# Softmax heads of a hybrid decoder layer: scores computed twice, per 512 queries, and no transposes of the weights

## The chip, the core and the metric

The kernel runs on one core of one Trainium2 chip. The metric is the device time of one execution in microseconds (us), the median of several runs. A core has a matrix engine (TensorE: PE for its matmuls, PEld for the weight loads of the same queue), VectorE (DVE), ScalarE (ACT), GpSimd (POOL) and SyncE (SP), which here issues the DMAs. Every engine works through its own list of instructions in order, and waits on semaphores for the others.

## The reference

One decoder layer over 2048 tokens of width 1024, in float32. A combined projection feeds four mixers: A stick-breaking attention (4 heads of 64), B a gated MLP, C an RWKV-7 recurrence, D forgetting attention (4 heads of 64). Their outputs go through `w_out`, then a mixture of 32 experts and a last norm. The change concerns D alone, which for each head computes

```python
logits = einsum('bhqd,bhkd->bhqk', q, k) * scale
logits = logits + cum[q] - cum[k]          # cumulative log forget gate
probs  = softmax(where(k <= q, logits, -inf))
out    = einsum('bhqk,bhkd->bhqd', probs, v)
```

## The kernel before

The program runs the input projection, then RWKV (C) together with the two attentions (A, then D), then the output projection with the router, then the experts. The order of the instructions on each engine is fixed when the program is built: a scheduler takes the code of RWKV and of the attentions and lays them into one another, so each engine's list in this part alternates between pieces of both. It knows no more than what the code's tiles depend on and its own idea of how long things take.

The softmax heads (D) are handled in blocks `b` of 256 queries, two tiles `i` of 128 queries each. For a tile the method `softmax` goes over the keys in pieces `c` of 512 (`spans`). `logits` writes a bank `z` of PSUM with queries on the partitions and keys along the row: one matmul of `qs` (stationary) with `kh`, one with `kl`, both float32r, and on the diagonal a 128-wide bf16 matmul (L378) that adds the mask. `kh` and `kl` are the rounded key and its remainder; `qs` holds the rounded query in its upper and the remainder in its lower 64 rows. One DVE operation (L402) scales the bank, adds the key's gate `nk`, writes the result `S` to SBUF and keeps the running maximum `m`. After the last piece two small DVE operations make the bias (L408, L409), ACT takes the exponential of every piece in place and sums the row (L413), and DVE forms the reciprocal (L416).

Then `weigh` treats the keys two tiles (`p`) at a time: three or four 128x128 transposes by the matrix engine (L425) bring the weights to keys on the partitions, ACT copies them to SBUF (`tq`, L427), and two float32 matmuls (L431) with the 64-wide `v` as stationary tile write the even keys to partitions 0 to 63 of `o` and the odd keys to 64 to 127. `out` adds the two halves and multiplies by the reciprocal, which two more transposes (L455) lay along the row. `logits` and `weigh` also serve the stick-breaking heads (A). While the matmuls of one block's `weigh` run, the next block's logits are made.

`load` brings a 512-token piece of `q`, `k`, `v` and the gate by DMA and splits them on POOL (L344, L345, L350, L351, L366).

Of the kernel before, what the change touches and what calls it, by code (L numbers as in the profile page):

```python
# [8 lines left out]
F32 = mybir.dt.float32  # L9
# [11 lines left out]
NT = 16  # L21
W = 256
NH = 4
# [284 lines left out]
def attention(tc, K, ctx, sT, sV, cumD, mixT):  # L308
# [13 lines left out]

    def bank():
        return ps.tile([128, 512], F32, name="bk", tag="bk")

    class Head:
        def __init__(self, h, sb):
            self.h, self.sb = h, sb
            self.q0, self.k0, self.v0 = (0, 256, 0) if sb else (512, 768, 256)
            self.q0, self.k0, self.v0 = (a + h * HD for a in (self.q0, self.k0, self.v0))  # L330
            self.kh, self.kl, self.qs, self.v, self.nk = [], [], [], [], []
            if sb:
                self.vc = cp.tile([64, NT], F32, name="vc", bufs=2)
                with nc.allow_non_contiguous_dma(reason="small"):
                    nc.sync.dma_start(self.vc, dram(sV, 127 * 516 + self.v0, [[1, HD], [128 * 516, NT]]))

        def load(self, c):
# [16 lines left out]
            if self.sb:  # L354
                u = rp.tile([128, 4, HD], F32, name="u")
# [15 lines left out]
        def logits(self, i, c, w):  # L371
            q = self.qs[i // 4][:, (i % 4) * 128:(i % 4) * 128 + 128]
            last = c == i // 4
            z = bank()
            nc.tensor.matmul(z[:, :w], q, self.kh[c][:, :w], start=True, stop=False)  # L375
            nc.tensor.matmul(z[:, :w], q, self.kl[c][:, :w], start=False, stop=not last)  # L376
            if last:
                nc.tensor.matmul(z[:, w - 128:w], K.identb, K.sb_mask if self.sb else K.fx_mask, start=False, stop=True)  # L378
            return z[:, :w]

        def spans(self, i):
            n = (i + 1) * 128
            return [(c, c * 512, min(512, n - c * 512)) for c in range(i // 4 + 1)]
# [11 lines left out]

        def softmax(self, i, S, rq):
            mx = None
            for c, x0, w in self.spans(i):
                z = self.logits(i, c, w)
                S[c] = sp.tile([128, 512], F32, name="S", tag="S")  # L400
                m = tp.tile([128, 1], F32, name="m")
                nc.vector.tensor_tensor_reduce(S[c][:, :w], z, self.nk[c][:, :w], 0.125,  # L402
                                               -3.0e38 if mx is None else mx, op0=OP.add, op1=OP.max, accum_out=m)
                mx = m
                yield
            c1 = cq[:, i, self.h:self.h + 1]
            bias = tp.tile([128, 1], F32, name="bias")
            nc.vector.tensor_add(bias, mx, c1)  # L408
            nc.vector.tensor_sub(bias, c1, bias)  # L409
            sm = tp.tile([128, 4], F32, name="sm")  # L410
            n = i // 4 + 1
            for c, x0, w in self.spans(i):
                nc.scalar.activation(S[c][:, :w], S[c][:, :w], AF.Exp, bias=bias, accum_out=sm[:, c:c + 1])  # L413
            if n > 1:
                nc.vector.tensor_reduce(sm[:, 0:1], sm[:, 0:n], AX.X, OP.add)
            nc.vector.reciprocal(rq, sm[:, 0:1])  # L416
# [17 lines left out]
        def out(self, b, o, rq):  # L434
            ol = op.tile([64, 256], F32, name="ol")
            oo = op.tile([64, 256], F32, name="oo")
            if self.sb:
                for a in range(2):
                    s = slice(a * 128, a * 128 + 128)
                    c = self.vc[:, 2 * b + a:2 * b + a + 1]  # L440
                    if a or b:
                        nc.scalar.activation(ol[:, s], o[64:128, s], AF.Identity, bias=c)
                    else:
                        nc.vector.tensor_copy(ol[:, s], c.to_broadcast([64, 128]))
                nc.vector.tensor_add(oo, o[0:64], ol)
                nc.sync.dma_start(mixT[self.h * HD:self.h * HD + HD, b * 256:b * 256 + 256], oo)
                return
            if b:
                nc.scalar.activation(ol, o[64:128], AF.Copy)
            else:  # L450
                nc.vector.memset(ol[:, 0:128], 0.0)
                nc.scalar.activation(ol[:, 128:256], o[64:128, 128:256], AF.Copy)
            t = bank()
            for a in range(2):
                nc.tensor.transpose(t[:, a * 128:a * 128 + 128], rq[:, a:a + 1].to_broadcast([128, 128]), K.ident)  # L455
            nc.vector.tensor_add(oo, o[0:64], ol)
            nc.vector.tensor_mul(oo, t[0:64, 0:256], oo)
            r0 = 768 + self.h * HD
            nc.sync.dma_start(mixT[r0:r0 + HD, b * 256:b * 256 + 256], oo)

        def block(self, b):
            S = [{}, {}]
            rq = None if self.sb else tp.tile([128, 2], F32, name="rq")
            o = []

            def weigh(p, first, last):
                if first:
                    o.append(po.tile([128, 256], F32, name="o"))
                self.weigh(b, p, S, o[0], first, last)
                if last:  # L470
                    self.out(b, o[0], rq)
# [14 lines left out]
            def front0():  # L486
                if b % 2 == 0:
                    self.load(b // 2)
                yield from self.softmax(2 * b, S[0], rq[:, 0:1])

            def mid():
                yield from self.softmax(2 * b + 1, S[1], rq[:, 1:2])

            def back0():
                for p in range(b + 1):
                    weigh(p, p == 0, p == b)
                    yield

            if self.sb:
                return [([front(c)], [], back(c)) for c in range(b // 2, -1, -1)]  # L500
            return [([front0()], [mid()], back0())]

    prev = iter(())
    for sb in (True, False):
        for h in range(NH):
            H = Head(h, sb)
            for b in range(8):
                for first, second, back in H.block(b):
                    for g in first:
                        yield from g  # L510
                    for g in second:
                        for _ in prev:
                            yield
                            next(prev, None)
                            next(g, None)
                        yield from g
                    yield from prev
                    prev = back
    yield from prev
# [1356 lines left out]
```

## Time and profile before

| | before |
|---|---|
| median of 3 runs (lowest to highest) | 2599.4 us (2596.69 to 2601.01) |
| profiled execution, first to last instruction | 2606.8 us |
| mean granted TensorE clock of it | 0.967 of full speed |
| busy share PE / PEld / DVE / ACT / POOL | 94% / 67% / 64% / 51% / 26% |

The times of the runs and the profiled execution are separate executions: the profiled one took 2606.8 us, 7.4 us (0.3%) over the median. A busy share is an average over stages with different limits. The softmax heads stand from about 1060 to 1522 us of the profiled execution, with RWKV's second half laid between them; the output projection's first matmul starts at 1526.3 us.

### The profile page before, as it was taken

To read this page: it belongs to the slowest core of one execution; us is meant where nothing else is said; L and a number is where in the kernel's file an instruction comes from. 1 tells how busy PE (TensorE), PEld (TensorE's weight loads), DVE (VectorE), ACT (ScalarE), POOL (GpSimd) and SP (SyncE) were. 2 spreads that over 40 slices of the span, in tenths; PEclk is the share of its full clock that TensorE was granted. 3 is DMA by queue.
4 is the path that set the end of the run, shared out by engine and by line. 5 is a ranking of instruction groups with operands and counts; after the bars stand their busy time and mean duration, and the time that the engine had idled before them with its cause. 6 is when DMAs were issued, how large, how long until landed. Compare 5 with 4: busy or idle time off the path is not lost. (4 is left out here: it accounts for less than half of the span.)

```text
span 2606.8 us, 42226 instructions
## 1 busy us (share of the span) xinstructions
PE 2442.3 (94%) x14802; PEld 1754.4 (67%) x14803; DVE 1675.3 (64%) x3881; ACT 1324.1 (51%) x2527; POOL 675.1 (26%) x691
## 2 busy tenths in 40 slices
PE   7999999997989898999999998997999999999994
PEld 6789998874656564656556667774666666676663
DVE  5313402247797869687685756665677787787885
ACT  5201222224655565675565642223667677776774
POOL 2000000015464647331332022112212232222224
PEclk9999999998989999999999999998999999999997
DMA  8510222125120211111111059443989899899995
GB/s 245 174 59 30 77 69 69 63 67 118 34 60 26 48 41 39 46 55 41 49 32 43 11 187 275 130 122 111 337 271 331 306 329 368 308 321 358 327 317 164
DMA packets 241826, 394.73 MB, mean 151 GB/s; under 512 B 65921, under 2 KB 106753, under 8 KB 241608
## 3 DMA queue, kind: packets, MB, share of 16 engines
q1 hardware_dynamic: 222472, 336.68, 39.1%
q0 software_dynamic: 19136, 55.30, 7.5%
q8 instruction: 118, 1.93, 0.3%
q14 instruction: 100, 0.82, 0.1%
HBM read 319.24 MB, written 76.85 MB: 152 GB/s over the span
## 5 line engine op out<-in xcount | busy, mean ns | idle before, releaser
L72 DVE TENSOR_TENSOR wl<-wr,wh 128x1024 fp32r<-128x1024 f32 x366 | 442.6, 1223 | 114.5 <-ACT wh L71 107.6
L71 ACT ACTIVATE wh<-wr 128x1024 fp32r<-128x1024 f32 x366 | 381.6, 1057 | 138.0 <-PE pg L1446 53.8
L393 DVE TENSOR_TENSOR_SCAN S<-S,zero 128x512 f32<-128x512 f32 (+3 forms) x160 | 197.8, 1246 | 50.5 <-POOL S L391 50.3
L152 PE MATMUL p<-hhi,wh 128*128 128x512 f32 x512 | 206.1, 404 | 14.8 <-ACT hhi L112 6.9
L425 PE MATMUL bk<-ident,S 128*128 128x128 f32 x1088 | 186.3, 292 | 24.5 <-DVE S L393 18.5
L427 ACT ACTIVATE tq<-bk 128x512 f32<-128x512 f32 (+1 forms) x288 | 156.6, 571 | 101.0 <-PE bk L425 81.4
L154 PE MATMUL p<-hhi,wl 128*128 128x512 f32 x512 | 205.2, 401 | 0.0
L153 PE MATMUL p<-hlo,wh 128*128 128x512 f32 x512 | 204.9, 400 | 0.0
L431 PE MATMUL o<-tq,v 128*64 128x256 f32 (+1 forms) x1152 | 189.3, 400 | 4.3 <-ACT tq L427 2.8
L425 PEld LDWEIGHTS bk<-ident,S 128*128 128x128 f32 x1088 | 124.0, 145 | 98.3 <-issue 53.4
L156 DVE TENSOR_TENSOR e<-p,rb 128x512 f32<-128x512 f32 x64 | 43.6, 689 | 198.3 <-PE p L154 183.9
L391 POOL TENSOR_SCALAR S<-S 128x512 f32<-128x512 f32 (+3 forms) x160 | 127.9, 808 | 145.8 <-ACT S L390 129.8
L735 POOL TENSOR_TENSOR k<-big,k 128x512 f32<-128x512 f32 x8 | 14.2, 1774 | 554.8 <-DVE big L734 548.8
L375 PE MATMUL bk<-kh,qs 128*128 128x512 f32 (+2 forms) x320 | 147.7, 462 | 7.2 <-POOL qs L351 4.8
L171 PE MATMUL p<-wh,hhi 128*128 128x256 f32 (+1 forms) x512 | 144.6, 282 | 0.0
L172 PE MATMUL p<-wl,hhi 128*128 128x256 f32 (+1 forms) x512 | 144.3, 282 | 0.0
L173 PE MATMUL p<-wh,hlo 128*128 128x256 f32 (+1 forms) x512 | 143.7, 281 | 0.0
L152 PEld LDWEIGHTS p<-hhi,wh 128*128 128x128 f32 x512 | 97.9, 191 | 40.2 <-ACT hhi L112 6.5
L413 ACT ACTIVATE S<-S,bias 128x512 f32<-128x512 f32 (+3 forms) x160 | 103.6, 649 | 34.2 <-DVE bias L409 33.7
L376 PE MATMUL bk<-kl,qs 128*128 128x512 f32 (+2 forms) x320 | 120.9, 379 | 0.0
L71 ACT ACTIVATE wh<-raw 128x512 fp32r<-128x512 f32 (+1 forms) x52 | 27.6, 589 | 179.2 <-PE p L153 171.7
L1443 PE MATMUL pg<-wh,xh 128*128 128x512 f32 x248 | 102.6, 414 | 12.6 <-ACT s L1450 12.6
(559 smaller groups left out, 6144.6 us busy)
## 6 DMA issues: line engine op xcount, KB each, us to landing
wr<-in SPq DMA_DIRECT2D x386, 512.0 KB
raw<-in SPq DMA_DIRECT2D x108, 256.0 KB
sT<-e SPq DMA_DIRECT2D x64, 256.0 KB
raw<-sT SPq DMA_DIRECT2D x128, 128.0 KB
mr<-mixT SPq DMA_DIRECT2D x16, 512.0 KB
xt<-in SPq DMA_DIRECT2D x16, 512.0 KB
xacc<-xt SPq DMA_DIRECT2D x16, 512.0 KB
h2D<-h SPq DMA_DIRECT2D x16, 512.0 KB
```

Of the source, the lines that this page charges most:

```text
L71: nc.scalar.activation(hi, raw, AF.Copy)
L72: nc.vector.tensor_sub(lo, raw, hi.bitcast(F32))
L152: nc.tensor.matmul(p, wh[:, k, ms], hi[j][:, k], start=(k == 0), stop=False)
L153: nc.tensor.matmul(p, wh[:, k, ms], lo[j][:, k], start=False, stop=False)
L154: nc.tensor.matmul(p, wl[:, k, ms], hi[j][:, k], start=False, stop=(k == KD - 1))
L171: nc.tensor.matmul(p, a, wh[:, k], start=first and k == 0, stop=False, skip_group_check=True)
L172: nc.tensor.matmul(p, a, wl[:, k], start=False, stop=False, skip_group_check=True)
L375: nc.tensor.matmul(z[:, :w], q, self.kh[c][:, :w], start=True, stop=False)
L393: nc.vector.tensor_tensor_scan(r, r, K.zero.to_broadcast([128, w]), 1.0 if c == i // 4 else S[c + 1][:, 0:1], op0=OP.mult, op1=OP.add)
L425: nc.tensor.transpose(t[:, x:x + 128], S[a][j // 4][:, (j % 4) * 128:(j % 4) * 128 + 128], K.ident)
L427: nc.scalar.activation(tq[:, :w], t[:, :w], AF.Copy)
L431: nc.tensor.matmul(o[64 * e:64 * e + 64, o0:256], self.v[j // 4][:, j % 4], tq[:, x0:x1], start=first, stop=last, skip_group_check=True)
```

## The change

The softmax heads leave `Head.softmax`, `weigh` and `out`, which now serve the stick-breaking heads alone, and become a class `Forget` that treats 512 queries (`Q`) of a head at a time, in two passes.

- Pass 1, `front`: the same logits as before, tile by tile of 128 queries; DVE keeps the maxima, and the other output (`junk`, bf16) is not used.
- `shift`: four transposes lay the 512 maxima along the row; ACT and DVE write them, as a rounded part and a remainder, into two of the lower rows of `qm`.
- Pass 2, `weights`: the logits once more, with the key tile as stationary tile and 512 queries (fewer on the diagonal) along the row. `kl` has ones in two of its lower rows, so that the second matmul also subtracts the maxima. ACT takes the exponential straight from PSUM into `P`, with the key's gate as bias `ncq`.
- `pair`: two matmuls of `v` with `P`, up to 512 queries wide, to the two halves of `o`; POOL adds the `P` tiles up in `acc`.
- `finish`: two matmuls with `ones` sum `acc` over the keys, DVE takes the reciprocals, and the output is formed as before.

The second pass of one `Q` is coded between the fronts of the next.

```diff
+    ncq = cp.tile([128, NT, NH], F32, name="ncq")
+    nc.vector.tensor_scalar(ncq, cq, -1.0, None, op0=OP.mult)
...
+    ones = cp.tile([128, 64], F32, name="ones")
...
-            nc.gpsimd.tensor_sub(kl, raw, kh.bitcast(F32))
+            if self.sb:
+                nc.gpsimd.tensor_sub(kl, raw, kh.bitcast(F32))
+            else:
+                nc.gpsimd.tensor_sub(kl[0:64], raw[0:64], kh[0:64].bitcast(F32))
+                nc.gpsimd.tensor_scalar(kl[64:128], raw[64:128], 0.0, pick[64:128], op0=OP.mult, op1=OP.add)
...
+            if not self.sb:
+                qm = hp.tile([128, 512], F32R, name="qm", bufs=2)
+                nc.gpsimd.tensor_scalar(qm, raw, upper, 0.0, op0=OP.mult, op1=OP.add)
+                self.qm.append(qm)
...
-        def softmax(self, i, S, rq):
...
+    class Forget:
...
+        def front(self, a, c):
+            H, Q = self.H, self.Q
+            w = 512 if c < Q else a * 128 + 128
+            s = slice(a * 128, a * 128 + 128)
+            z = bank()
+            nc.tensor.matmul(z[:, :w], self.qs[:, s], H.kh[c][:, :w], start=True, stop=False)
+            nc.tensor.matmul(z[:, :w], self.qm[:, s], H.kl[c][:, :w], start=False, stop=c < Q)
+            if c == Q:
+                nc.tensor.matmul(z[:, w - 128:w], K.identb, K.fx_mask, start=False, stop=True)
+            junk = rp.tile([128, 512], BF, name="u", tag="u")
+            m = self.m[:, a:a + 1] if c == Q else tp.tile([128, 1], F32, name="mc")
+            nc.vector.tensor_tensor_reduce(junk[:, :w], z[:, :w], H.nk[c][:, :w], 0.125, -3.0e38 if c == 0 else self.mx,
+                                           op0=OP.add, op1=OP.max, accum_out=m)
+            self.mx = m
+
+        def shift(self):
+            t = bank()
+            for a in range(4):
+                nc.tensor.transpose(t[:, a * 128:a * 128 + 128], self.m[:, a:a + 1].to_broadcast([128, 128]), K.ident)
+            low = self.qm[96:128]
+            nc.scalar.activation(self.qm[64:128], t[64:128], AF.Copy, scale=-8.0)
+            nc.vector.scalar_tensor_tensor(low, t[96:128], -8.0, low.bitcast(F32), op0=OP.mult, op1=OP.subtract)
...
+        def weights(self, j):
+            H, x = self.H, self.x0(j)
+            c, s = j // 4, slice(j % 4 * 128, j % 4 * 128 + 128)
+            diag = j >= 4 * self.Q
+            z = bank()
+            nc.tensor.matmul(z[:, x:], H.kh[c][:, s], self.qs[:, x:], start=True, stop=False)
+            nc.tensor.matmul(z[:, x:], H.kl[c][:, s], self.qm[:, x:], start=False, stop=not diag)
+            if diag:
+                nc.tensor.matmul(z[:, x:x + 128], K.fx_mask, K.identb, start=False, stop=True)
+            P = sp.tile([128, 512], F32, name="S", tag="S")
+            nc.scalar.activation(P[:, x:], z[:, x:], AF.Exp, scale=0.125, bias=ncq[:, j, H.h:H.h + 1])
+            self.P[j] = P
+
+        def pair(self, j0):
...
+            for j in (j0, j0 + 1):
+                x = self.x0(j)
+                e = 64 * (j - j0)
+                nc.tensor.matmul(self.o[e:e + 64, x:], H.v[j // 4][:, j % 4], self.P[j][:, x:], start=j0 == 0, stop=last,
+                                 skip_group_check=True)
+            for j in (j0, j0 + 1):
...
+                elif j:
+                    nc.gpsimd.tensor_add(self.acc[:, x:], self.acc[:, x:], self.P[j][:, x:])
+            if last:
+                self.finish()
+
+        def finish(self):
+            t = bank()
+            for e in range(2):
+                nc.tensor.matmul(t[64 * e:64 * e + 64, 0:256], ones, self.acc[:, 256 * e:256 * e + 256], start=True, stop=True,
+                                 skip_group_check=True)
...
+            for e in range(2):
+                nc.vector.reciprocal(rs[:, 256 * e:256 * e + 256], t[64 * e:64 * e + 64, 0:256])
...
+            nc.scalar.activation(ol[:, x:], self.o[64:128, x:], AF.Copy)
+            nc.vector.tensor_add(oo, self.o[0:64], ol)
+            nc.vector.tensor_mul(oo, rs, oo)
...
+        def backs(self):
+            n = 4 * self.Q + 4
+
+            def step(j):
+                for i in (j, j + 1):
+                    if i < n:
+                        self.weights(i)
+                if j:
+                    self.pair(j - 2)
+
+            return [lambda j=j: step(j) for j in range(0, n + 2, 2)]
...
+    for h in range(NH):
+        H = Head(h, False)
+        for Q in range(4):
+            H.load(Q)
+            F = Forget(H, Q)
+            f, n = F.fronts(), 0
+            for i, g in enumerate(f):
+                g()
+                yield
...
+                while n * len(f) < (i + 1) * len(rest):
+                    rest[n]()
+                    n += 1
+                    yield
```

The scheduler decides where each of these stands. On the matrix engine of the kernel before, at the end of a block of a softmax head, the list reads as follows (L375, L376, L378 are logits and mask, L425 the transposes of the weights, L431 the two matmuls with `v`, L455 the transposes of the reciprocals, L913 belongs to RWKV).

```order
L431 MATMUL o_15090<-tq_15154,v_14546 64x256 x2
L375 MATMUL bk_15185<-kh_15062,qs_15069 128x384
L376 MATMUL bk_15185<-kl_15063,qs_15069 128x384
L378 LDWEIGHTS identb_71
L378 MATMUL bk_15185<-fx_mask_77,identb_71 128x128
L431 MATMUL o_15090<-tq_15163,v_14777 64x256 x2
L425 MATMUL bk_15199<-ident_68,S_15081 128x128
L425 MATMUL bk_15199<-ident_68,S_15113 128x128 x2
L431 MATMUL o_15090<-tq_15171,v_14777 64x256
L431 MATMUL o_15090<-tq_15171,v_14777 64x128
L455 MATMUL bk_15211<-ident_68,rq_15058 128x128 x2
L913 MATMUL bk_8958<-qt_8972,M0_8988 64x128 x2
```

The two matmuls with `v` stand next to each other. In the list of the changed kernel the same work looks so (lines of the changed file: L482 and L483 are the logits of pass 1, L485 their mask, L508 and L509 those of pass 2, L525 the matmuls with `v`):

```order
L525 MATMUL o_13886<-S_13934,v_13454 64x512
L482 MATMUL bk_13959<-kh_13841,qs_13851 128x512
L525 MATMUL o_13886<-S_13939,v_13454 64x512
L483 MATMUL bk_13959<-kl_13842,qm_13849 128x512
L485 LDWEIGHTS identb_71
L485 MATMUL bk_13959<-fx_mask_77,identb_71 128x128
L508 MATMUL bk_13965<-qs_13625,kh_13615 128x512
L509 MATMUL bk_13965<-qm_13623,kl_13616 128x512
```

Here a logits matmul stands between the two matmuls of one pair. Another place of the changed kernel, on the same engine, some 280 places on, has the second half of a pair more than ten places behind the first, with an RWKV merge (L914, L916) and logits between:

```order
L525 MATMUL o_14378<-S_14398,v_14036 64x512
L914 MATMUL bk_8812<-ident_68,xc_8666 128x128
L916 MATMUL bk_8812<-bd321_4722,xc_8666 32x128 x4
L482 MATMUL bk_14415<-kh_14147,qs_14331 128x512
L483 MATMUL bk_14415<-kl_14148,qm_14329 128x512
L482 MATMUL bk_14421<-kh_14321,qs_14331 128x256
L483 MATMUL bk_14421<-kl_14322,qm_14329 128x256
L485 LDWEIGHTS identb_71
L485 MATMUL bk_14421<-fx_mask_77,identb_71 128x128
```

The second half comes five places after the last of these. Over the whole list, the pairs with `v` of the softmax heads stood next to each other in the kernel before in all but 1 of 144 cases; in the changed kernel they do in 27 of 80, and 53 are split. The two matmuls with `ones` (16 pairs) are split in 12.

## Rows read from the trace of the kernel before

**Rows 1.** Busy time by stretch: window, length, then busy us (instructions) per engine.
```profile
core 0: us, PE busy (x) PEld busy (x) DVE busy (x) ACT busy (x) POOL busy (x), PEclk, DMA share, GB/s
620.00:1060.00 440.00, 399.04 (x2888) 251.05 (x2888) 362.69 (x594) 261.18 (x616) 251.88 (x255) 0.94 0.21 51
1060.00:1515.00 455.00, 443.65 (x3416) 282.11 (x3417) 313.98 (x1090) 281.94 (x766) 108.64 (x114) 0.99 0.14 39
```

**Rows 2.** Groups by line and form, 1060 to 1515 us: busy us, mean ns, idle before.
```profile
L431 PE MATMUL o<-tq,v 128*64 128x256 f32 x506 | 93.5, 404 | 0.9 <-ACT tq L427 0.8
L425 PE MATMUL bk<-ident,S 128*128 128x128 f32 x543 | 88.0, 285 | 3.4 <-DVE m L402 2.9 <-ACT S L413 0.2
L413 ACT ACTIVATE S<-S,bias 128x512 f32<-128x512 f32 x112 | 79.8, 714 | 29.8 <-DVE bias L409 29.4
L427 ACT ACTIVATE tq<-bk 128x512 f32<-128x512 f32 x112 | 62.9, 593 | 38.3 <-PE bk L425 30.4 <-PE o L431 6.6
...
L402 DVE CUSTOM_DVE_ANT_0 S<-bk,nk,m 128x512 f32<-128x512 f32 x60 | 44.2, 737 | 21.9 <-PE bk L376 14.1 <-PE bk L378 7.5
...
L413 ACT ACTIVATION_READ_ACCUMULATOR S<-S,bias 128x1 f32 x160 | 30.2, 189 | 0.0
L837 DVE TENSOR_TENSOR xe<-bk,b 128x512 f32<-128x512 f32 x40 | 27.1, 677 | 4.7 <-PE bk L834 4.6
```

**Rows 3.** PE's timeline in the softmax stage: start us, us, engine line op names.
```profile
1495.92 0.65 PE L431 MATMUL o<-tq,v 128*64 128x256 f32 x4
1496.51 0.50 PE L375 MATMUL bk<-kh,qs 128*128 128x512 f32 x1
1496.84 0.40 PE L376 MATMUL bk<-kl,qs 128*128 128x512 f32 x1
1497.17 0.65 PE L431 MATMUL o<-tq,v 128*64 128x256 f32 x4
1497.75 0.66 PE L425 MATMUL bk<-ident,S 128*128 128x128 f32 x4
1498.34 0.65 PE L431 MATMUL o<-tq,v 128*64 128x256 f32 x4
1498.92 0.66 PE L425 MATMUL bk<-ident,S 128*128 128x128 f32 x4
1499.51 0.33 PE L913 MATMUL bk<-qt,M 64*64 64x128 f32 x2
```

**Rows 4.** PE's timeline at the end of a block, on the diagonal.
```profile
1414.18 0.34 PE L376 MATMUL bk<-kl,qs 128*128 128x384 f32 x1
1414.36 0.23 PE L378 MATMUL bk<-fx_mask,identb 128*128 128x128 bf16 x1
1414.52 0.65 PE L431 MATMUL o<-tq,v 128*64 128x256 f32 x4
1415.10 0.55 PE L425 MATMUL bk<-ident,S 128*128 128x128 f32 x3
1415.58 0.43 PE L431 MATMUL o<-tq,v 128*64 128x256 f32 x2
```

**Rows 5.** PE's timeline where float32r matmuls follow one another (input projection).
```profile
99.81 0.39 PE L152 MATMUL p<-hhi,wh 128*128 128x512 f32 x1
...
101.21 0.39 PE L152 MATMUL p<-hhi,wh 128*128 128x512 f32 x1
```

**Rows 6.** PE's timeline where the two matmuls of one pair stand apart.
```profile
1063.49 0.65 PE L431 MATMUL o<-tq,v 128*64 128x256 f32 x2
1064.07 0.68 PE L870 MATMUL bk<-xtf,y 64*64 64x64 f32 x8
1064.68 0.65 PE L431 MATMUL o<-tq,v 128*64 128x256 f32 x2
1065.25 0.49 PE L892 MATMUL bk<-rbT,wz 128*128 128x128 f32 x2
```

**Rows 7.** PE's timeline in the experts: 64-column float32 pairs, 512 wide.
```profile
1893.46 2.31 PE L1551 MATMUL pgu<-wr,x2t 128*64 128x512 f32 x10
1895.71 0.50 PE L1443 MATMUL pg<-wh,xh 128*128 128x512 f32 x1
```

**Rows 8.** POOL's groups by line and form, 1060 to 1515 us.
```profile
L351 POOL TENSOR_TENSOR qs<-raw,qs 64x512 fp32r<-64x512 f32 x15 | 20.2, 1344 | 1.2
...
L350 POOL TENSOR_SCALAR qs<-raw 128x512 fp32r<-128x512 f32 x14 | 8.7, 621 | 134.8 <-PE bk L378 129.1 <-PE bk L376 5.6
...
L743 POOL TENSOR_TENSOR r<-r,k 128x512 f32<-128x512 f32 x3 | 4.8, 1592 | 0.0
...
L741 POOL TENSOR_TENSOR bkt<-a,ec 128x512 f32<-128x512 f32 x3 | 4.0, 1332 | 0.0
```

More of the change, by code (lines that the diff above doesn't have):

```diff
@@ L321, in attention @@
             nc.sync.dma_start(cq[:, :, h], cumD[h].rearrange("(i p) -> p i", p=128))
+    ncq = cp.tile([128, NT, NH], F32, name="ncq")
+    nc.vector.tensor_scalar(ncq, cq, -1.0, None, op0=OP.mult)
+    upper = cp.tile([128, 1], F32, name="upper")
+    nc.gpsimd.memset(upper, 0.0)
+    nc.gpsimd.memset(upper[0:64], 1.0)
+    pick = cp.tile([128, 1], F32, name="pick")
+    nc.gpsimd.memset(pick, 0.0)
+    nc.gpsimd.memset(pick[64:65], 1.0)
+    nc.gpsimd.memset(pick[96:97], 1.0)
+    ones = cp.tile([128, 64], F32, name="ones")
+    nc.gpsimd.memset(ones, 1.0)
     def bank():
@@ L377, in logits @@
             if last:
-                nc.tensor.matmul(z[:, w - 128:w], K.identb, K.sb_mask if self.sb else K.fx_mask, start=False, stop=True)
+                nc.tensor.matmul(z[:, w - 128:w], K.identb, K.sb_mask, start=False, stop=True)
             return z[:, :w]
-        def spans(self, i):
-            n = (i + 1) * 128
-            return [(c, c * 512, min(512, n - c * 512)) for c in range(i // 4 + 1)]
         def sticks(self, i, c, S):
@@ L432, in weigh, with out @@
                                  start=first, stop=last, skip_group_check=True)
-        def out(self, b, o, rq):
+        def out(self, b, o):
             ol = op.tile([64, 256], F32, name="ol")
             oo = op.tile([64, 256], F32, name="oo")
[L437 to L453, printed above, removed]
-            for a in range(2):
-                nc.tensor.transpose(t[:, a * 128:a * 128 + 128], rq[:, a:a + 1].to_broadcast([128, 128]), K.ident)
+            for a in range(2):
+                s = slice(a * 128, a * 128 + 128)
+                c = self.vc[:, 2 * b + a:2 * b + a + 1]
+                if a or b:
+                    nc.scalar.activation(ol[:, s], o[64:128, s], AF.Identity, bias=c)
+                else:
+                    nc.vector.tensor_copy(ol[:, s], c.to_broadcast([64, 128]))
             nc.vector.tensor_add(oo, o[0:64], ol)
-            nc.vector.tensor_mul(oo, t[0:64, 0:256], oo)
-            r0 = 768 + self.h * HD
-            nc.sync.dma_start(mixT[r0:r0 + HD, b * 256:b * 256 + 256], oo)
+            nc.sync.dma_start(mixT[self.h * HD:self.h * HD + HD, b * 256:b * 256 + 256], oo)
         def block(self, b):
             S = [{}, {}]
-            rq = None if self.sb else tp.tile([128, 2], F32, name="rq")
             o = []
@@ L484, in back @@
                     yield
[L486 to L496, printed above, removed]
-                    yield
-            if self.sb:
-                return [([front(c)], [], back(c)) for c in range(b // 2, -1, -1)]
@@ L501, in block @@
[L501 to L518, printed above, removed]
@@ new lines, in attention @@
+    prev = iter(())
+    for h in range(NH):
+        H = Head(h, True)
+        for b in range(8):
+            for front, back in H.block(b):
+                yield from front
+                yield from prev
+                prev = back
+    rest = None
+    for h in range(NH):
+        H = Head(h, False)
[6 more added lines that the diff above has]
+                yield
+                if rest is None:
+                    next(prev, None)
+                    continue
+                while n * len(f) < (i + 1) * len(rest):
+                    rest[n]()
+                    n += 1
+                    yield
+            if rest is None:
+                yield from prev
+            rest = F.backs()
@@ L522 @@
+    for g in rest:
+        g()
+        yield
 CK = 128
```

58 lines of the change are left out of this document (33 added, 25 removed).

## Prediction

> **What bounds the kernel now.** I read the busy time by stretch first, because the engines' shares over the whole span mix stages. In the stretch of the softmax heads the matrix engine is busy 443.65 of 455 us at a granted clock of 0.99; DVE 313.98, ACT 281.94 and POOL 108.64 us [rows 1]. So PE has 11 us of idle time there, and no other engine is near it. The groups by line then show whose time that is: matmuls with `v` (L431) and transposes (L425) lead, and their idle time before them is 0.9 and 3.4 us; ACT and DVE wait for PE, not PE for them (38.3 us of L427's idle time, most of it ended by L425) [rows 2]. RWKV's second half shares the list, so the stretch ends when PE has done the work of both, and what matters is how much PE time the change adds or removes.
>
> For that the mean durations in the groups are no use: matmuls are pipelined, and a duration holds the time to drain. The price of an operation is its **slot**: from its start to the start of what follows. In the softmax stage two adjacent matmuls with `v` take 0.59, 0.58, 0.58 us, the two logits matmuls 0.33 each, four transposes 0.59 and 0.59 [rows 3]. Three transposes take 0.48, a mask 0.16 with the switch to `v` behind it [rows 4].
>
> **The change part by part, on PE.** Per head the softmax weights make 36 `weigh` calls, 8 of them with three transposes.
>
> *Transposes of the weights go.* 112 x 0.59 + 32 x 0.48 = 81 us less. A reader who took the mean duration of 285 ns [rows 2] would write 544 x 0.285 = 155 us; the slots say 147 ns.
> The Trainium skill (TensorE: Matmul & The Clock Gate, Part 4: PE-mode transpose) gives a transpose about 275 ns in a kernel's context; by that the removal would be worth 150 us. The rows differ: four of them share 0.59 us, so 275 is what one takes, not what one costs in a stream.
>
> *The second pass's logits come.* It streams the same columns as the first: 17,408 per head for `kh` and again for `kl`, over four heads as much as 272 matmuls of 512. Where float32r matmuls follow one another, six take from 99.81 to 101.21, 0.233 us each [rows 5]: 63 us. Between other work a pair of them takes 0.67 instead of 0.47 [rows 3], so a run of float32r costs 0.2 us for entering and leaving. In the order of the changed kernel I count 255 such runs in this stage, before 141: 114 x 0.2 = 23 us. 64 more masks at 0.07 (0.16 less the switch, already counted): 5 us. Together 91 us; the bounds are 68 (no new switches) and 112 x 0.67 + 48 narrower at 0.5 + 64 x 0.16 = 109.
>
> *The matmuls with `v` change.* Before, 144 pairs at 0.58 = 84 us. The new pairs are up to 512 wide, with the same columns in all, so if each pair stood together they would cost less: ten instructions of that width, which run two at a time, take 2.25 us, 0.45 per slot of two [rows 7], so a pair (each float32 matmul is two instructions) 0.9, or 1.0 with the switches at both ends; 64 such pairs and 16 narrow ones at 0.58 make 73 us. But a pair is cheap only because its two halves, which use different 64 columns of the array, run at the same time. Where the kernel before has the halves of one pair apart, each takes 0.58 us, from 1063.49 to 1064.07 and from 1064.68 to 1065.25 [rows 6]: the pair costs double. The order of the changed kernel splits 53 of 80 pairs. Its 106 lone halves are 77 of 512 columns (1.0 us each), 11 of 384 (0.8), 9 of 256 (0.58), 9 of 128 (0.36), 94 us; the 27 pairs left are 20 wide and 7 narrow, 24 us. So 118 us, 34 more than before.
> The Trainium skill (TensorEngine Tiling (Array Packing), Key Properties) says the same of both sides: different tiles work in parallel, and a change of tiling mode drains the array. Rows 3 and 6 agree; no sum hangs on it.
>
> *The sums by `ones` come.* 16 pairs of 256 columns like L431's; 12 are split in the order. 24 x 0.58 + 4 x 0.58 = 16 us. The 64 transposes of `shift` replace the 64 of the reciprocals (L455): nothing.
>
> PE: -81 + 91 + 34 + 16 = **+60 us**.
>
> **The other engines.** ACT loses the copies of L427 (62.9 us for the wide ones alone) and 30.2 us of row sums [rows 2]; an exponential that reads PSUM is not in the trace, and lies between the 593 ns of the copy from PSUM and the 714 ns of the one before [rows 2]. That is covered by PE either way. DVE keeps its 160 maxima and loses the small operations on biases. The 32 reciprocals of 64x256 are not in the trace either; at ten times 0.4 us they would add 130 us to 314 in a stage of over 500, which still does not bind. POOL gains most: 96 additions of 128x512 at 1.33 to 1.59 us [rows 8] and 48 narrower ones, some 180 us, and two more operations per `load` at 0.62 [rows 8], 20 us; about 310 us of 520, behind PE on average. No DMA is added to `load`.
>
> *New waits.* The second pass of a `Q` cannot start before `shift`: last maximum 0.74, a transpose 0.15 (of a slot of four), ACT 0.59, DVE 0.68 [rows 2, 3], then the matmul with `qm`: 2.2 us, 16 times, 35 us if nothing covers it. Behind it on PE stand further fronts and RWKV's matmuls, and in the order two or more microseconds of such work lie between the last front and the first matmul with the finished `qm` where I looked. Likewise `ones` waits for POOL's last addition, with 16 places. I take 5 us of the 0 to 60 that both could cost.
>
> Sum: 2606.8 + 65 = 2672 for an execution like the profiled one, whose span is 7.4 us over the median of the runs; against the median, 2599.4 + 65 = **2664 us**.
>
> **Rivals.**
> *Transposes cost what they last.* This is the case on the other side: if removing them frees 0.285 us each [rows 2], because PE's queue is held for all of it, the sum is -155 + 91 + 34 + 16 + 5 = -9, 2590 us. It decides from 0.27 us per transpose. Against it stand the starts that follow [rows 3]. The skill's 275 ns would land beside it, with the sum at -4. Chance 0.08.
> *Split halves overlap after all.* If only the time between the halves changes and both still share the array, `v` costs 73 and `ones` 9: -81 + 91 - 11 + 9 + 5 = +13, 2612 us. [rows 6] speaks against it, on one case. With the logits at their lower bound as well, 23 less, it reaches the range of no change. Chance 0.13.
> *POOL or the new waits bind.* If POOL's additions hold back `ones`, the buffers `S` and RWKV's own POOL work (products of 1.33 and 1.59 us [rows 8]), every one of 16 boundaries stalls PE by 3 to 5 us instead of 0.3: 45 to 75 us more, 2710 to 2740. For it: POOL's load rises threefold, and its list is in order. Against: it has 200 us of slack on average.
> The Trainium skill (GPSIMD Engine Reference, Engine selection) advises VectorE for additions with two inputs and calls GpSimd about twice as slow; the rows agree, 1.33 to 1.59 us against DVE's 0.68 for 128x512 [rows 2, 8]. Chance 0.16.
>
> **How the numbers follow.** The forecast has 0.63, of which its own spread (logits 68 to 109, waits 0 to 35) is 2636 to 2700. The range from 2606 to 2714 takes in most of the second rival and the lower end of the third; outside remain the first rival, the lower part of the second and most of the third, about 2 in 10. A change under 0.2% (5 us) is what a measurement of this kernel hardly tells from none. Faster: the first rival and a little of the second, 0.10. Same: part of the second, 0.05. Slower: 0.85.
>
> **What the profile after would show.** The output projection's first matmul would start near 1590 instead of 1526 us. PE would still be busy over 95% of the stage. The starts around a lone half with `v` 512 wide would lie 0.9 to 1.0 us apart, and those of an adjacent pair too. The logits groups would have 320 matmuls each instead of 160, at about the same mean price. POOL would be near 300 us in the stage. The prediction is wrong if a lone half takes about 0.5 us, if PE's idle time in the stage is well over 20 us, or if the stretch before 1060 us or after the output projection moves by more than a few microseconds.

## The result, and the profile after

The changed kernel is slower: 2730.17 us (median of 4 runs, 2728.9 to 2737.6) against 2598.05 (4 runs, 2596.34 to 2601.01), a ratio of 1.0506 with an interval of 1.0486 to 1.0526. The forecast was 2664, in a range from 2606 to 2714. The profiled executions differ by 2728.6 - 2606.8 = 121.8 us. I call the time from the first mask of the softmax logits to the first matmul of the output projection the **stage**: 1059.7 to 1526.3 before, 1046.9 to 1644.9 after, so 466.6 and 598.0 us, 131.4 more. The stick-breaking heads ahead of it end 12.8 us earlier, and what lies behind it takes 3.1 us more.

The busy time by stretch of the changed kernel, to be read against [rows 1]:

```profile
core 0: us, PE busy (x) PEld busy (x) DVE busy (x) ACT busy (x) POOL busy (x), PEclk, DMA share, GB/s
...
1060.00:1150.00 90.00, 83.39 (x447) 47.88 (x445) 71.17 (x170) 31.46 (x73) 40.04 (x38) 0.91 0.08 21
1150.00:1250.00 100.00, 92.74 (x519) 54.79 (x518) 58.49 (x134) 36.53 (x87) 51.14 (x56) 0.84 0.18 49
1250.00:1350.00 100.00, 95.79 (x557) 48.99 (x556) 61.62 (x147) 33.15 (x73) 58.44 (x57) 0.94 0.12 33
1350.00:1450.00 100.00, 89.10 (x523) 48.66 (x522) 81.95 (x190) 37.89 (x93) 51.07 (x51) 0.95 0.09 26
1450.00:1550.00 100.00, 95.78 (x580) 53.70 (x578) 59.48 (x148) 34.34 (x80) 50.88 (x55) 0.95 0.12 32
1550.00:1645.00 95.00, 78.11 (x380) 39.35 (x379) 44.36 (x91) 30.70 (x59) 33.31 (x60) 0.91 0.18 55
```

Two things are to be seen. PE was busy 97.5% of its time, now 82 to 96%, and the granted clock, 0.99 before, is 0.84 to 0.95. DVE's share is 64% on average after 69, POOL's 49 after 24: neither looks like a bound.

The groups by line of the stage (answering [rows 2] and [rows 8]), then what PE waited for in it:

```profile
L534 POOL TENSOR_TENSOR tq<-tq,S 128x512 f32<-128x512 f32 x84 | 108.4, 1291 | 59.5 <-ACT S L513 56.8
L525 PE MATMUL o<-S,v 128*64 128x512 f32 x224 | 107.6, 634 | 0.5 <-DVE S L550 0.5
...
L508 PE MATMUL bk<-qs,kh 128*128 128x512 f32 x112 | 57.3, 513 | 9.4 <-DVE S L545 8.4 <-ACT S L513 1.0
L482 PE MATMUL bk<-kh,qs 128*128 128x512 f32 x112 | 56.7, 506 | 3.7 <-DVE mc L488 3.3 <-ACT S L513 0.3
L545 DVE RECIPROCAL S<-bk 64x256 f32<-64x256 f32 x32 | 56.0, 1751 | 5.9 <-PE bk L541 4.5 <-ACT y L948 1.2
```

```profile
PE p L1185 <- ACT wh L1131: 10.7, 1, 10.7
PE bk L508 <- DVE S L545: 10.3, 7, 2.5
PE bk L482 <- DVE mc L488: 4.8, 7, 2.0
PE bk L509 <- DVE qm L498: 3.4, 5, 1.0
PE bk L495 <- DVE m L488: 3.4, 6, 1.4
```

Apart from the one at the end of the stage (L1185), the largest end with DVE: with the reciprocals (L545), or with maxima and a shift (L488, L498), which share its list. POOL ends none of the larger ones. One such place, DVE's and PE's timeline:

```profile
1517.42 3.52 DVE L545 RECIPROCAL S<-bk 64x256 f32<-64x256 f32 x2
1517.44 0.54 PE L495 MATMUL bk<-ident,m 128*128 128x128 f32 x3
1517.74 0.48 PE L482 MATMUL bk<-kh,qs 128*128 128x512 f32 x1
1518.05 0.40 PE L483 MATMUL bk<-kl,qm 128*128 128x512 f32 x1
...
1520.99 0.50 PE L508 MATMUL bk<-qs,kh 128*128 128x512 f32 x1 [2.54 <-DVE S L545]
```

The two reciprocals of a `finish` hold DVE's list for 3.52 us. PE has 1 us of work left and then waits: by the trace, L508 starts when a reciprocal has ended, so the bank that it is to write is one that the reciprocals read. The granted clock, in the windows around it:

```profile
1510.00:1518.00 8.00, 7.67 (x53) 4.48 (x54) 7.96 (x20) 1.89 (x6) 3.74 (x5) 1.00 0.08 17
1518.00:1521.70 3.70, 0.95 (x3) 0.20 (x2) 3.65 (x4) 0.00 (x0) 0.00 (x0) 1.00 0.00 0
1521.70:1531.00 9.30, 8.84 (x31) 4.14 (x32) 6.21 (x19) 2.54 (x4) 2.53 (x2) 0.50 0.07 15
1531.00:1540.00 9.00, 9.00 (x59) 4.23 (x58) 5.15 (x15) 1.96 (x3) 2.69 (x3) 0.95 0.01 2
```

PE works at full clock, waits 2.54 us, and is then granted half (1.2 of 2.4 GHz) for some 10 us, although it is busy again. What that costs is seen on lone halves with `v`, two instructions each, a little apart (another place, with the clock of the two stretches below):

```profile
1250.41 1.88 PE L525 MATMUL o<-S,v 128*64 128x512 f32 x2
1252.22 0.50 PE L508 MATMUL bk<-qs,kh 128*128 128x512 f32 x1
...
1252.87 1.07 PE L525 MATMUL o<-S,v 128*64 128x512 f32 x2
1253.88 0.50 PE L482 MATMUL bk<-kh,qs 128*128 128x512 f32 x1
```

```profile
1246.00:1252.00 6.00, 6.00 (x22) 3.23 (x22) 5.32 (x14) 3.03 (x7) 3.77 (x3) 0.50 0.60 147
1252.00:1262.00 10.00, 10.00 (x55) 5.07 (x54) 5.66 (x21) 3.49 (x10) 3.32 (x4) 1.00 0.02 5
```

The same work has a slot of 1.81 us in a stretch at half clock and of 1.01 at full.

### The profile page after: what moved, and what is told of

It is laid out like the page before. It is cut to its first block, busy times and chain, and to the rows that moved or that the text cites. A ratio compares the mean times of both kernels' runs of the same rounds, so it can differ in the third digit from the quotient of the medians.

```text
span 2728.6 us, 41349 instructions
## 1 busy us (share of the span) xinstructions
PE 2529.8 (93%) x14450; PEld 1763.7 (65%) x14451; DVE 1738.5 (64%) x3658; ACT 1245.0 (46%) x2223; POOL 857.4 (31%) x877
## 5 line engine op out<-in xcount | busy, mean ns | idle before, releaser
L409 DVE TENSOR_TENSOR_SCAN S<-S,zero 128x512 f32<-128x512 f32 (+3 forms) x160 | 206.0, 1298 | 37.6 <-POOL S L407 37.1
L513 ACT ACTIVATE S<-bk,ncq 128x512 f32<-128x512 f32 (+3 forms) x160 | 95.2, 622 | 161.0 <-PE bk L509 92.4
L534 POOL TENSOR_TENSOR tq<-tq,S 128x512 f32<-128x512 f32 (+3 forms) x128 | 140.3, 1096 | 83.2 <-ACT S L513 79.3
L525 PE MATMUL o<-S,v 128*64 128x512 f32 (+3 forms) x320 | 130.7, 568 | 0.5 <-DVE S L550 0.5
L1185 PE MATMUL p<-wh,mh 128*128 128x512 f32 x256 | 103.9, 410 | 18.6 <-ACT wh L1131 10.7
L419 PE MATMUL bk<-ident,S 128*128 128x128 f32 x544 | 97.5, 296 | 24.2 <-DVE S L409 22.1
L153 PEld LDWEIGHTS p<-hlo,wh 128*128 128x128 f32 x512 | 97.1, 190 | 24.3 <-issue 1.1
L154 PEld LDWEIGHTS p<-hhi,wl 128*128 128x128 f32 x512 | 96.9, 189 | 23.8 <-issue 0.7
```

The lines of the kernel that those rows point to most:

```text
L153: nc.tensor.matmul(p, wh[:, k, ms], lo[j][:, k], start=False, stop=False)
L154: nc.tensor.matmul(p, wl[:, k, ms], hi[j][:, k], start=False, stop=(k == KD - 1))
L409: nc.vector.tensor_tensor_scan(r, r, K.zero.to_broadcast([128, w]), 1.0 if c == i // 4 else S[c + 1][:, 0:1], op0=OP.mult, op1=OP.add)
L525: nc.tensor.matmul(self.o[e:e + 64, x:], H.v[j // 4][:, j % 4], self.P[j][:, x:], start=j0 == 0, stop=last, skip_group_check=True)
L534: nc.gpsimd.tensor_add(self.acc[:, x:], self.acc[:, x:], self.P[j][:, x:])
```

## The experiments

All results are ratios to the kernel before on the same chip. The table gives, for the stage of each profiled execution: its length; PE's slots (start to next start, less the waits); PE's waits; and the time at half clock in the trace's record of the granted clock. These four come from one execution each, and whole executions of one kernel on one chip lie up to 17 us apart, so a few us between two stages mean nothing.

| run | median us | ratio (interval) | stage | slots | waits | half clock |
|---|---|---|---|---|---|---|
| before | | | 466.6 | 451.9 | 14.7 | 11.9 |
| after | 2730.2 | 1.0506 (1.0486 to 1.0526) | 598.0 | 547.9 | 50.1 | 99.3 |
| e1_pairs | 2711.2 | 1.0429 (1.0395 to 1.0463) | 582.2 | 510.8 | 71.4 | 145.8 |
| e2_recip | 2717.1 | 1.0459 (1.0431 to 1.0487) | 589.2 | 556.7 | 32.5 | 110.9 |
| e3_both | 2678.3 | 1.0310 (1.0282 to 1.0337) | 551.0 | 509.0 | 42.0 | 116.6 |
| e5_tail | 2678.5 | 1.0288 (1.0265 to 1.0312) | 548.1 | 509.9 | 38.1 | 115.8 |
| e4_norecip | stage only | | 553.4 | 520.7 | 32.7 | 40.8 |
| e6_nosum | stage only | | 557.9 | 527.3 | 30.6 | 65.9 |
| e7_neither | stage only | | 537.7 | 514.2 | 23.6 | 23.6 |
| e8_bothnosum | stage only | | 518.6 | 487.2 | 31.4 | 49.6 |
| e9_memset | stage only | | 566.1 | 530.3 | 35.8 | 69.9 |
| b1_recip | 2663.6 | 1.0222 (1.0195 to 1.0249) | 523.3 | 481.9 | 41.4 | 71.7 |
| b5_half | 2637.2 | 1.0136 (1.0112 to 1.0161) | 495.1 | 462.7 | 32.4 | 38.9 |
| b2_serial | 2657.5 | 1.0200 (1.0171 to 1.0229) | 526.3 | 503.3 | 23.0 | 23.9 |
| b3_pool | 2631.7 | 1.0117 (1.0094 to 1.0141) | 495.7 | 463.0 | 32.7 | 36.0 |
| b7_memset | 2607.3 | 1.0011 (0.9999 to 1.0023) | 468.4 | 450.3 | 18.0 | 13.7 |
| b6_lessdve | 2614.8 | 1.0034 (1.0021 to 1.0048) | 474.3 | 452.7 | 21.6 | 19.6 |

"Stage only" marks kernels that leave out part of the denominators. Their outputs are other numbers, and with them the experts' work can change (behind the stage `e4_norecip` takes 1577 us, the changed kernel 1084), so only the stage is compared.

**Parts of the change: pairs kept together.** The first matmul of a pair waits for both exponentials, the first with `ones` for the last addition.

```diff
+            self.exps[j] = nc.scalar.activation(P[:, x:], z[:, x:], AF.Exp, ...)
...
+                if j == j0:
+                    wait_for(tc, mm, [self.exps[j0 + 1]])
```

> Against the changed kernel (2730 us). The first matmul of each pair with v, and the first of the two with ones, now waits for what the second one needs, so that the scheduler lays both halves next to each other (all 80 pairs and all 16, by the order). Theory lone halves: v falls from 122 us of PE slots to about 80 and ones from 18 to about 10, so the time falls by some 45 to 55 us, to about 2680. Rival halves overlap anyway: the time stays within 10 us of 2730. Rival waits: holding the first half back costs more idle time on PE than it saves, 2730 or more.

The matmuls with `v` of the softmax heads fall from 120 to 78 us of slots, those with `ones` from 18 to 13: the price of apart halves is close to the forecast. But of these 47 us only 19 reach the median, which lies between the theory (2680) and the rival (within 10 us of 2730). Waits rise by 21 us and the time at half clock by 46, which other slots pay for, so that all slots fall by 37 only. The longer slots seem to have covered waits; no run shows that by itself.

**Narrow reciprocals.** The sums are formed on the partitions (128x1 matmuls), 128x4 reciprocals taken, and these transposed as the kernel before did.

```diff
+                nc.tensor.matmul(t[:, a:a + 1], self.acc[:, a * 128:a * 128 + 128], ones[:, 0:1], ...)
+            nc.vector.reciprocal(rq, t[:, 0:4])
+                nc.tensor.transpose(t[:, a * 128:a * 128 + 128], rq[:, a:a + 1].to_broadcast([128, 128]), K.ident)
```

> Against the changed kernel (2730 us). The sums over the keys come out with queries on the partitions (four one-column matmuls), DVE takes the reciprocal of 128x4, and four transposes lay it along the row, in place of 32 DVE reciprocals of 64x256 at 1.75 us. Theory DVE blocks PE: the idle time of PE after the reciprocals and maxima (some 20 us) goes and with it part of the time at the low clock, 2685 to 2710. Rival POOL: the reciprocals hide behind PE, and four more transposes and four small matmuls cost 1 us 16 times: 2725 to 2745.

Waits fall by 18 us, but slots rise by 9, the size of the 64 new transposes: 13 us in the median, 2717 us, between the two ranges.

**Both edits.**

> Both edits together. If lone halves and DVE's reciprocals are separate costs, the gains add up: 2635 to 2665. If the second only shows because PE is late, no more than the first alone, about 2680.

52 us come back, more than the two apart (19 + 13). The median lies above the range for separate gains (2635 to 2665); 2680 was named for the first edit alone, which had reached only 2711, so neither reading foretold it. That each edit had left what the other removes would fit, and is not shown further.

**The reciprocals alone taken away**: a copy of the same shape stands in their place, so the output is multiplied by the sums instead of divided.

```diff
-                nc.vector.reciprocal(rs[:, 256 * e:256 * e + 256], t[64 * e:64 * e + 64, 0:256])
+                nc.vector.tensor_copy(rs[:, 256 * e:256 * e + 256], t[64 * e:64 * e + 64, 0:256])
```

> The changed kernel with the 32 reciprocals left out: a DVE copy of the sums stands in their place (the weights are multiplied by their sum instead of divided). Theory DVE blocks PE: 2685 to 2710, like the cheaper reciprocals, without their PE work. Rival POOL: 2725 to 2735.

The copy takes 417 ns where the reciprocal took 1751, so DVE is 43 us lighter, and the stage 44.6 us shorter: 17 us of waits, and 27 of slots, with 58 us less at half clock.

**The end of the stage.** In the kernel with both edits, the last head's last write of `mixT` goes through ACT's queue; in the changed kernel the loads of `w_out` (`wr`, which ACT turns into `wh`) stand behind it on SP.

```profile
1639.30 0.45 SPq L553 DMA_DIRECT2D mixT<-S  x1
1639.79 4.71 SPq L1130 DMA_DIRECT2D wr<-in  x8
```

> The kernel with paired halves and narrow reciprocals, and the last head's last write of mixT issued from ACT's queue instead of SP's, so that the loads of w_out don't stand behind it on SP. If that place in SP's order is what the first matmul of the output projection waits for at the end (10.7 us for wh in the changed kernel, 6.3 in the one with both edits), the wait falls to 2 us or less and the median from 2678 to about 2673. Rival: the loads wait for the release of buffers by the last heads' work on PE, POOL and DVE anyway; then nothing moves (2676 to 2680).

A miss: the wait for `wh` falls from 6.3 to 2.5 us, the median does not move, as the rival had it. In the changed kernel itself, where that wait is 10.7 us (nothing in the kernel before), the edit was not tried.

**POOL's additions left out** for keys before the diagonal (72 of 84 wide ones).

```diff
-                elif j:
+                elif j > max(0, 4 * self.Q - 1):
```

> The changed kernel without POOL's additions of weights for keys before the diagonal: 72 of 84 wide additions at 1.29 us are left out, 93 us of POOL, so the denominators are wrong, and only the stage from the first softmax logits to the output projection is read (598 us in the changed kernel). My theory (DVE's reciprocals and the clock that falls after the waits): the stage stays within 8 us, 590 to 606. Rival of the prediction, POOL holds back the sums and the buffers S: the stage loses 20 to 45 us, 553 to 578, and PE's idle time falls from 50 us towards 20.

My theory failed here: the stage lost 40 us, as the rival had it, although in the changed kernel PE never waits for POOL, and ACT for 8 us only. Ten of the 40 lie at the stage's end, where the wait for `wh` falls from 10.7 to 0.6 us; with the reciprocals taken away it was 8.0.

**The same edits put into the kernel before**, where one load at a time can be added with the output unchanged. First its reciprocals, as 64x256 from PSUM:

```diff
-            nc.vector.reciprocal(rq, sm[:, 0:1])
+            nc.vector.tensor_copy(rq, sm[:, 0:1])
...
+            nc.vector.reciprocal(rs, t[0:64, 0:256])
+            nc.vector.tensor_mul(oo, rs, oo)
```

> The kernel before with the changed kernel's choice of reciprocal alone: the row sums are transposed and the reciprocal is taken of 64x256 from PSUM, 32 times at about 1.75 us, instead of 64 of 128x1. DVE rises from 314 to about 368 of 455 us in the stretch. My theory: an in-order DVE makes PE wait for maxima and products behind each reciprocal, so PE's idle time rises from 15 to 25 to 45 us and the granted clock of the stretch falls below 0.97; 2610 to 2640 us. The prediction's view (DVE has slack, PE covers it): 2596 to 2604.

```profile
L458 DVE RECIPROCAL rs<-bk 64x256 f32<-64x256 f32 x32 | 55.8, 1744 | 17.4 <-PE bk L455 17.2
```

```profile
1060.00:1515.00 455.00, 419.21 (x3053) 266.68 (x3052) 330.59 (x1038) 251.12 (x691) 105.32 (x107) 0.93 0.13 36
```

61 us, more than I had put at the top. DVE is busy 331 of 455 us, PE only 419 (444 in [rows 1]), and the clock is 0.93: the 56 us of reciprocals are passed on whole, half as waits (27 us of the stage), half as slower slots (30).

Both halves of a pair with `v` in the same 64 columns, so that they can't run together:

```diff
+                r = 64 * e if self.sb else 0
-                nc.tensor.matmul(o[64 * e:64 * e + 64, o0:256], ...
+                nc.tensor.matmul(o[r:r + 64, o0:256], ...
```

> The kernel before with both matmuls of each pair with v into the same 64 columns of the softmax heads' output, so that the two can't run at the same time; nothing else moves. If the price of an operation is its slot on PE and a pair is cheap only because its halves share the array, a pair's slot goes from 0.58 to about 1.03 us and the kernel is 144 x 0.45 = 65 us slower, 2664 (2645 to 2685), with no new waits and a granted clock still at 0.98 or above. Rival: the halves hardly overlap, or other work covers them: under 2620.

```profile
1313.53 1.08 PE L432 MATMUL o<-tq,v 128*64 128x256 f32 x4
1314.54 0.65 PE L425 MATMUL bk<-ident,S 128*128 128x128 f32 x4
1315.13 1.08 PE L432 MATMUL o<-tq,v 128*64 128x256 f32 x4
```

A pair's slot is 1.01 instead of 0.58 us [rows 3]; the slots with `v` rise by 53 us, the median by 55. PE's slots are the price, here about one to one; waits rise by 8 us, which was not announced, and the clock in the stretch of [rows 1] is 0.97, not 0.98 or above.

POOL's additions, one for each piece of a row, whose result is not used. They are 160, where the changed kernel has 144, so the load is a little larger (181 us on POOL against 160):

```diff
+                nc.gpsimd.tensor_add(self.acc[:, :w], self.acc[:, :w], S[c][:, :w])
```

> The kernel before with the changed kernel's load on POOL alone: each row of exponentials is also added into one tile on POOL, 160 additions with the same columns as the changed kernel's (17,408 per head, some 170 us at 1.29 us for 128x512), whose result is not used. POOL rises from 109 to about 280 of 455 us in the stretch. By the prediction POOL has slack and nothing moves: 2595 to 2608. By the rival (the buffers S come free later, POOL's own work for RWKV and for load comes later) 25 to 45 us more: 2625 to 2645.

And half of the reciprocals' length, 32 of 64x128 (945 ns each, 30 us):

> The kernel before with half of what cost 61 us there: the reciprocals of 64x256 are taken for the even query tile only, 32 of 64x128 at about 0.88 us. If DVE's list is short of time as a whole, or each stall is passed on in full, the cost is half, 25 to 32 us: 2625 to 2635. If the work that PE has ahead in its four banks covers a stall of under one microsecond and only the long one gets through, it is under 12 us: 2600 to 2612.

Both cost: 32 us for POOL's additions, 37 for half the reciprocals (61 for all), a little over the range for half. So the short stall is not covered by work that PE has ahead; the cost goes with DVE's added time. How POOL's additions do it is seen in DVE's groups, first of the kernel before, then with the additions:

```profile
L408 DVE TENSOR_TENSOR bias<-m,cq 128x1 f32<-128x1 f32 x64 | 18.8, 294 | 0.5
L847 DVE COPY_PREDICATED xc<-lev,tw 128x128 f32<-128x128 int32 x32 | 12.0, 382 | 0.1
```

```profile
L402 DVE CUSTOM_DVE_ANT_0 S<-bk,nk,m 128x512 f32<-128x512 f32 x60 | 44.2, 736 | 13.8 <-PE bk L378 6.3 <-PE bk L376 5.7 <-issue 1.0
...
L411 DVE TENSOR_TENSOR bias<-m,cq 128x1 f32<-128x1 f32 x62 | 23.7, 383 | 0.4
L851 DVE COPY_PREDICATED xc<-lev,tw 128x128 f32<-128x128 int32 x32 | 21.3, 678 | 0.1
```

DVE's operations on two SBUF operands last longer, 678 instead of 382 ns for the same copy under a mask (`COPY_PREDICATED`); the maxima, which read PSUM, do not (736 against 737 in [rows 2]). In the other variants of the kernel before, without additions, that copy has 365 to 462 ns. Two operands are not the whole of it: three copies of 128x512 within SBUF (L684, here L688) go from 415 to 1199 ns. DVE is busy 349 instead of 314 of 455 us, for work that the edit has not touched. That POOL gives the buffers `S` back later is not the cause: DVE waits 1.0 us in all for POOL to have read one.

**POOL's time without its reads**: three memsets (together some 1.37 us for 512 columns) in place of each addition, behind the same exponential `e`. The cut is against the run with the additions.

```diff
-                nc.gpsimd.tensor_add(self.acc[:, :w], self.acc[:, :w], S[c][:, :w])
+                wait_for(tc, nc.gpsimd.memset(self.acc[:, :w], 0.0), [e])
+                nc.gpsimd.memset(self.acc[:, :w], 0.0)
+                nc.gpsimd.memset(self.acc[:, :w // 2], 0.0)
```

> The kernel before with POOL's load as in the run with the 160 extra additions (about 1.3 us per 512 columns, each started behind the same exponential), but made of memsets, which read nothing. If POOL's additions cost through DVE, whose operations on two SBUF operands they hold up, DVE's copy_predicated goes back from 678 to about 382 ns and the time from 2632 to 2597 to 2608 us. If POOL's time and its in-order list cost, it stays at 2620 to 2640.

```profile
L853 DVE COPY_PREDICATED xc<-lev,tw 128x128 f32<-128x128 int32 x32 | 11.3, 365 | 0.1
```

```profile
1060.00:1515.00 455.00, 439.92 (x3387) 278.82 (x3387) 316.30 (x1085) 278.06 (x761) 298.80 (x592) 0.98 0.14 38
```

POOL is busier than with the additions (299 against 278 us), DVE is back at 316, and the time is that of the kernel before (0.1% more, with an interval up to 0.23%). In this kernel POOL's additions cost through DVE, and not by POOL's own time.

**The same in the changed kernel**: five memsets of 208 columns for each of the 72 additions.

> The changed kernel with each of the 72 additions for keys before the diagonal replaced by five memsets of 208 columns on POOL (about 1.3 us in all, behind the same exponential), so that POOL's time stays and its reads of SBUF go; the denominators are wrong, and only the stage is read (598 us in the changed kernel, 558 without the additions). If the additions cost through DVE alone, the stage is near 558, 550 to 568. If POOL's time costs, near 598, 588 to 605. In between, both do.

566.1 us: of the 40 us that went with the additions, 32 stay away when POOL's time is put back without its reads. DVE's busy time in the stage is 381 us in the changed kernel, 362 here and 358 without the additions. So some 20 of the 32 us are DVE's own; ten are the wait for `wh` again (0.5 us here), and why that one goes is open.

**Both loads out of the changed kernel**, and POOL's out of the one with both edits:

> The changed kernel with a copy in place of each 64x256 reciprocal and without POOL's additions for keys before the diagonal (the outputs are wrong by both; only the stage from the first softmax logits to the output projection is read: 598 us in the changed kernel, 553 with the copy alone, 558 without the additions alone). If the prediction's sum for PE was right and only these two loads were missed, the stage comes to 466.6 + 60 = 527 us, within 8: PE idle under 25 us and hardly any time at half clock. If the two edits repair the same waits, so that something else is still missing, it stays at 545 to 553.

> The kernel with paired halves and narrow reciprocals (stage 551 us), without POOL's additions for keys before the diagonal (denominators wrong; only the stage is read). If POOL's additions hold work back of themselves, the stage loses 20 to 40 us again, 511 to 531. If they cost only together with the wide reciprocals, it stays within 8 us of 551.

537.7 us, 11 above the 527 that PE's sum gives, so over the announced 8 and under the 545 of the other reading. Its slots are 514.2 us where the forecast has 451.9 + 60 = 511.9; the rest is waits, 23.6 us against 14.7. The second kernel loses 32 us again: POOL's additions cost without the wide reciprocals too.

**Less of DVE in the kernel before**: minus the maximum as bias, from ACT.

```diff
-            c1 = cq[:, i, self.h:self.h + 1]
...
-            nc.vector.tensor_add(bias, mx, c1)
-            nc.vector.tensor_sub(bias, c1, bias)
+            nc.scalar.activation(bias, mx, AF.Copy, scale=-1.0)
```

> The kernel before with 30 us less on DVE: the two operations for each row's bias (0.30 and 0.18 us, 64 times) become one on ACT, minus the maximum (the same softmax, rounded otherwise). If DVE's time is passed on one to one in this stage, as it was when 28 and 61 us were added, 2570 to 2580. If PE bounds the stage from below, with 15 us of idle time and 12 us at half clock left in it, 2588 to 2600.

Nothing is gained (0.3% slower; DVE at 296 and ACT at 292 us in the stretch): time added to DVE was passed on, but in this one test, which moves the work to ACT, time taken away did not come back. Of the versions of the change with its whole output, none beats the kernel before; the best, with both edits, has slots 57 us over it, with 117 us of the stage at half clock.

## Why the prediction was right and wrong

**PE's sum was right, in part by luck.** With the two missed loads out (`e7_neither`), PE's slots are 62 us more than before (60 forecast): the slots with `v` are 117 us (118), with `ones` 17 (16), the second logits 87 and their masks 7 (91 together), the weights' transposes 73 less (81). These parts come to some 70; that the first pass's logits are 5 us cheaper than before was in no term. Lone halves 512 wide cost 1.01 us (1.0), told from the 256-wide ones of [rows 6], and where halves were kept from sharing the array the time rose by their slots.

**The step that failed** is the one on the other engines. Of DVE's reciprocals the prediction says "which still does not bind", of POOL's additions "behind PE on average", and so neither has a term in the sum. "I take 5 us of the 0 to 60 that both could cost" is for `shift` and `ones` alone, and that was about right: PE waits some 7 us for the last maxima and for `qm` (L495, L509), and not at all for POOL's last addition. The stage missed its forecast of 466.6 + 65 by 66 us: taking the reciprocals out gives back 45, the additions 40, and both 60, since the two gains overlap. Seen from PE, 36 of the 66 are slots over the sum, with 99 us of the stage at half clock, and 30 are waits over the five, 10.7 of them the one at the end for `wh`.
The size was not the fault: I allowed ten times 0.4 us for a reciprocal, and it takes 1.75, 56 us in all. The fault was to ask whether an engine at 70% can become the bound. In this stage PE's list depends on DVE every few microseconds (160 maxima alone in 598 us, each of which frees a bank), so what DVE takes longer comes out as waits of PE, and behind most of the longer waits it runs some microseconds at half clock.

**The rival "POOL or the new waits bind"** had the size (2710 to 2740) and named POOL, but the size by luck: it left out the reciprocals, and its mechanism was another, `ones`, the buffers `S` and RWKV's POOL work held back. Of such waits PE shows none and ACT 8 us. POOL does its harm by its reads of SBUF, which lengthen DVE's operations within SBUF; shown in the kernel before by additions against memsets of the same length.
The Trainium skill (SBUF — State Buffer, SBUF: two separate sides) has this rule: GpSimd and VectorE share one pair of ports, which one of them takes for a whole instruction, and a VectorE operation with two SBUF inputs is held up only by GpSimd operations that read SBUF. The two runs with POOL's load agree: the copy under a mask goes from 382 to 678 ns with additions and is at 365 with memsets, and the maxima, with one input from PSUM, are unchanged.

**The other rivals** fell: transposes gave back 73 us and not 155; adjacent halves share the array (1.01 against 0.58 us a pair), apart ones don't.

**What was to be seen.** Announced were a first output matmul near 1590 us (1644.9), PE busy over 95% (82 to 96%), POOL near 300 us (some 285 in the rows above) and lone halves 0.9 to 1.0 us apart (1.01 at full clock). Signs of error were idle time "well over 20 us" and another stretch moving: idle time is 50 us, and the stick-breaking heads end 12.8 us earlier. In the variants of both kernels the stage starts anywhere from 1042.6 to 1059.7 us; why is left open, and it hid 13 us of the loss.

## What to carry over

A busy share says which engine can bind, not whose time is free: where PE's list passes through another engine every few instructions, price that engine's additions at about one to one (in the kernel before 30 us of reciprocals cost 37, 56 cost 61), with the clock that PE loses behind its waits in it, and treat cover by PE as unproven until a run with that load alone shows it. Price a new instruction by its length in the list of its engine, and look at what it does to its neighbours: additions given to POOL because POOL is idle lengthened DVE's operations here. To find such a cost, put each new load by itself into the old kernel, where the output and all else stay the same.

## What was not expected of the hardware

A 64x256 reciprocal from PSUM takes 1751 ns on DVE, a copy of the same shape 417; at 64x128 it is 945. Of 14 waits of PE of 1 us or more inside the stage of the changed kernel, nine were followed within 3.3 us by 3 to 10 us at half clock, with PE busy again; two fell into such a stretch and three were followed by none. Of the four other stretches, one begins in the wait at the stage's end and three (the longest of 17 us) stand behind no wait of that length. And a 128x128 copy under a mask on DVE went from 382 to 678 ns by nothing but additions on POOL.
